# Gated output rows of both mixer branches by a seven-product scheme, with one weight sum made by an accumulating DMA

## The chip, the cores and the metric

The kernel runs on one core of one Trainium2 chip. The metric is the device time of one execution in microseconds; the time before is the median of 3 runs, 2480.94 us (2480.85 to 2481.19). The profile is of one more execution of the same program.

## The reference

Two layers of a streaming encoder for 640 frames (512 of a prompt, 8 x 16 of running streams), 1024 wide. What is computed in each layer:

```
x += 1/2 * SwiGLU_1(RMSNorm(x))
h  = RMSNorm(x);  z = h @ w_in        # conv B | conv C | conv V | q | k | v | gates
y_c = B * causal_depthwise_conv3(C * V)                 # 512 channels
y_a = chunk-band attention(q, k, v)                     # 8 heads x 64
m  = sigmoid(g_c) * (y_c @ w_conv_out) + sigmoid(g_a) * (y_a @ w_attn_out)
x += m @ w_o
x += 1/2 * SwiGLU_2(RMSNorm(x))
```

The part at issue is the line of m: the 2 x 1024 gate columns of h @ w_in, two products with 512-deep weights, and the gating.

## The kernel before, in words

Activations lie with channels on the 128 partitions and the 640 frames in the free dimension, as two halves t1 and t2 of 320. Each product of float32 matrices is made from three: each operand is split into a rounded "hi" part (a cast, on ScalarE) and the rest "lo" (a subtraction, on VectorE), and hi x hi, hi x lo and lo x hi are added up in PSUM. So each weight tile takes three matmuls of 320 columns for each half of the frames.

**Weights.** They come in slabs of 128 x 1024 (512 KB) from one packed tensor, wst. SP loads each into one of three buffers called raw (L292, in load). prep (L351) casts a slab to whi on ScalarE (L364) and leaves the subtraction for wlo pending; flush (L369) issues it on VectorE. A slab is prepared about two ahead of its use.

**Seven products.** A part of the products uses a Strassen-Winograd scheme on 2 x 2 blocks: seven block products in place of eight, with sums of weights and of activations as operands. A unit of it (kind "mix" in the plan) takes two raw slabs, ra and rb, and prepares four slabs of weights out of them (source, L302 on): ra whole; the sums s = (rb first half + rb second half) + ra first half, and rb's own sum, as one slab; then a sum that was *lent*, beside a changed second half of ra; then the second half of rb. A lent sum is made by DMA: lend_one (L278) has POOL load half of ra into a buffer called one (L281) and then, when that has landed, has POOL add half of rb onto it (L282, a DMA that accumulates). There are two such buffers. Units with a lent sum are called lean; in the others VectorE makes that sum as well. In the lean units VectorE makes rb's own sum first (raw<-raw), then s (s<-raw,raw).

**The order.** In this stage the instructions of TensorE, VectorE and ScalarE run in the order in which the program writes them; those of POOL and SP are placed by a scheduler, and each queue then runs in its order. A wait of one instruction holds everything behind it on its engine. In the function outputs (L1497 on) each layer goes through gate pairs (gate_pair, two rows of 128 gates, seven blocks of twelve matmuls) with output rows in between: `out` makes one row of 128 as a plain product (24 matmuls, PSUM tile py), rows makes four rows at once by seven products (84 matmuls, tiles raco, rbco, rcco or the like). The order is: gate pair 2, plain rows 0 to 3 of the convolution branch, gate pairs 4 and 6, its rows 4 to 7 by seven, gate pair 8, two plain rows of the attention branch, gate pair 10, two more, gate pairs 12 and 14, its rows 4 to 7 by seven, then the output projection (tile po).

A gate pair of name m uses PSUM tiles qa, qb, qc out of four such banks in turn, so the second tile of a gate pair takes the bank of the first tile of the gate pair ahead of it. Each block's result is copied out by ScalarE or added up by VectorE (g<-qb, g<-qa, g<-qc) and multiplied with the row norms (L1541, L1548, L1554); the sigmoids follow a unit later (L1354). `ahead` in a gate pair or in rows, behind the fifth block, makes the next unit's weight sums: there VectorE meets raw<-raw and s<-raw,raw.

The branch results y_c and y_a are split into hi and lo whole for the plain rows, and their sums for the seven products are made in further tiles (xhico, xhiao).

Of the kernel before, what the change touches and what calls it, by code (L numbers as in the profile page):

```python
# [16 lines left out]
P = 128  # L17
# [179 lines left out]
def trunk(ctx: ExitStack, tc: tile.TileContext, xin, wst, small, pbias, samplebias, kcache, vcache, gfin,  # L197
# [64 lines left out]
    lent, lean, at = {}, set(), 0  # L262
    for name, (_, units) in zip([f"{k}{l}" for l in range(L) for k in "amb"], stages()):
# [5 lines left out]
        lean.update(ns[slice(*LEAN.get(name, (FREE, None)))])  # L269

# [13 lines left out]
    def load(i):  # L284
        while len(raws) <= i:
# [6 lines left out]
            SP.dma_start(raw, wst[n])  # L292
        return raws[i]
# [8 lines left out]
    def source(i):  # L302
# [3 lines left out]
        if i not in sources:  # L306
# [8 lines left out]
            else:  # L315
# [8 lines left out]
                elif arg == 1 and n in lean:  # L324
# [4 lines left out]
                    add(rb[:, h1], rb[:, h1], rb[:, h2])  # L329
# [1167 lines left out]
    def outputs(l, gp, X, st, cs, ycp, yas, sigmoid, gates):  # L1497
# [4 lines left out]
        ycs = [z[:, i] for z in ycp for i in range(2)]  # L1502
        mm = [spare[i // 2][:, i % 2] for i in range(CT)] + ycs
# [14 lines left out]
        def gate_pair(m, at):  # L1518
# [6 lines left out]
            u, g = gates[m], gates[m + 1] = tmp(f"g{n}"), tmp(f"g{n}_1")  # L1525
            prep(used[0] + 1)
            flush()
            at[0]()
# [8 lines left out]
            at[1]()  # L1537
# [6 lines left out]
            at[2]()  # L1544
# [11 lines left out]
            flush()  # L1556

        def parts(pool, tag, name, src):
            hi, lo = (pool.tile([P, T], F32R, tag=f"{tag}{i}", name=f"{name}{i}") for i in ("hi", "lo"))
            split(hi, lo, src)  # L1560
            return hi, lo

        def out(m, y, then=None, post=None):

            due()
            py = acc(f"py{l}_{m}")
            product(py, y)
            if then:
                then()
            g = gates[m]  # L1570
            if m < KT:
                DVE.tensor_tensor(out=halves(mm[m]), in0=two(py), in1=halves(g), op=ALU.mult)
            else:
                DVE.tensor_tensor(out=halves(g), in0=two(py), in1=halves(g), op=ALU.mult)
                add(mm[m - KT], mm[m - KT], g)
            flush()
            if post:
                post()

        yc, ya = [], []  # L1580
        mo = [None] * KT
        srcs = [yas[:, c, :] for c in range(CT)]
        x, moves = {}, []

        def take(y, name, cs, srcs):
            for c in cs:
                y.append(parts(gp, f"y{c}", f"{name}{l}_{c}", srcs[c]))

        def take_even(c):
            y = tuple(gp.tile([P, T], F32R, tag=f"y{c}{i}", name=f"ya{l}_{c}{i}") for i in ("hi", "lo"))  # L1590
            split(*(z[:, t1] for z in y), srcs[c][:, t1])
            ya.append(y)

        def low(lo, z, hi):
            DVE.tensor_tensor(out=lo, in0=z, in1=hi.bitcast(F32), op=ALU.subtract)

        def room(name):
            for k in EXTRA:
                x[name, k] = tuple(gp.tile([P, 2, HT], F32R, tag=f"x{EXTRA.index(k)}{i}",
                                           name=f"x{i}{name}{l}_{EXTRA.index(k)}") for i in ("hi", "lo"))  # L1600

        def minus(out, a):
            DVE.scalar_tensor_tensor(out=out, in0=a, scalar=-1.0, in1=out, op0=ALU.mult, op1=ALU.subtract)

        def mixed(i):

            z = ycp[i].rearrange("p c (a b) -> p (c a) b", a=2)
            e1, e2, o1, o2 = (z[:, k] for k in range(4))
            add(e1, e1, e2, ALU.subtract)
            add(e2, o2, e2, ALU.subtract)  # L1610
            minus(o2, e1)
            minus(o1, o2)
            yield
            for k in EXTRA:
                ACT.copy(x["co", k][0][:, i], z[:, 1 + EXTRA.index(k)])
            yield
            for k in EXTRA:
                hi, lo = (u[:, i] for u in x["co", k])
                low(lo, z[:, 1 + EXTRA.index(k)], hi)
            yield  # L1620
            hi, lo = (u[:, t2] for u in yc[2 * i])
            ACT.copy(hi, e1)
            yield
            low(lo, e1, hi)
            yield

        za = yas.rearrange("p (i c) (a b) -> p i (c a) b", i=2, a=2)

        def mix(n):

            e1, e2, o1, o2 = (za[:, :, k] for k in range(4))
            if n == 0:
                add(e1, e1, e2, ALU.subtract)
            elif n == 1:
                add(e2, o2, e2, ALU.subtract)
            else:
                minus(*((o2, e1) if n == 2 else (o1, o2)))

        def place(k):
            if k == XT5:  # L1640
                return [(*(u[:, t2] for u in ya[2 * i]), za[:, i, 0]) for i in range(2)]
            return [(*x["ao", k], za[:, :, 1 + EXTRA.index(k)])]

        def high(*ks):
            for k in ks:
                for hi, _, z in place(k):
                    ACT.copy(hi, z)

        def rest(*ks):
            for k in ks:  # L1650
                for hi, lo, z in place(k):
                    low(lo, z, hi)

        EXTRA = XT7, XT4, XN6

        def kind(name, i, k):
            if k in EXTRA:
                return tuple(z[:, i] for z in x[name, k])
            hi, lo = (yc if name == "co" else ya)[2 * i + (k in (X21, X22))]
            return tuple(z[:, t2 if k in (X22, XT5) else t1] for z in (hi, lo))  # L1660

        def rows(name, ms, first, mid=None, late=None, end=False, defer=False):

            n = f"{name}{l}_{ms[0]}"
            gs = [gates[m + (KT if name == "ao" else 0)] for m in ms]
# [3 lines left out]
            s1, s2, s5 = stage  # L1669

            def mul(ps, s, half, k, start):
                for u in range(2):
                    for i in range(2):
                        kp = half * NP + 2 * u + i
                        wh, wl = (z[:, kp * P : (kp + 1) * P] for z in s)
                        xh, xl = kind(name, i, k)
# [13 lines left out]
            def moved(r):  # L1690
                for u in range(2):
                    ACT.copy(mm[ms[2 * r + u]], gs[2 * r + u])

            w = quiet()
            mul(a, w, 0, X11, True)
            ACT.copy(s1, two(A))
# [3 lines left out]
            if first:  # L1700
                first()
            mul(b, w, 1, X21, True)
            add(s1, two(B), s1)
            w = slab(True)[0]
            flush()
# [3 lines left out]
            if mid:  # L1709
                mid()  # L1710
# [728 lines left out]
```

## Time and profile before

| what | value |
|---|---|
| median of 3 runs | 2480.94 us |
| the profiled execution, its span | 2479.9 us |
| TensorE (PE) busy | 2466.4 us, 17264 matmuls recorded |
| VectorE (DVE) busy | 2182.6 us |
| ScalarE (ACT) busy | 1386.7 us |
| POOL busy | 320.8 us |
| the changed stage, layer 0 and layer 1 | 139.30 us and 139.38 us |

Busy time is a share of the whole span; a wait shows only in the stage in which it stands. In rows of the profile "out<-in" names the tile written and those read, "xN" counts instructions, and L364 is line 364 of the kernel. "idle before <-X" is how long the engine had waited, and for whom. A DMA's landing time counts from its issue. The granted clock of TensorE is 1.00 throughout.

### The profile page before, as it was taken

How to read it: one execution, taken by the hardware profiler on the slowest of the kernel's cores; microseconds unless marked ns; L12 is line 12 of the kernel's file. 1: busy time of each engine (PE TensorE's matmuls, PEld its weight loads, DVE VectorE, ACT ScalarE, POOL GpSimd, SP SyncE). 2: the span in 40 equal slices, each digit the busy share in tenths (PEclk: the TensorE clock that was granted, in tenths of full speed). 3: DMA queues.
4: the chain of work that ended last, by engine and by line, in shares of the span. 5: the costliest groups of instructions: out<-in, count | busy, mean ns of one | idle time of the engine just before them, and what ended most of it. 6: DMA issues, size and time to landing. Idle time of an engine off the chain costs nothing.

```text
span 2479.9 us, 44056 instructions
## 1 busy us (share of the span) xinstructions
PE 2466.4 (99%) x17264; PEld 2414.6 (97%) x17264; DVE 2182.6 (88%) x3644; ACT 1386.7 (56%) x2231; POOL 320.8 (13%) x483
## 2 busy tenths in 40 slices
PE   9999999999999999999999999999999999999999
PEld 8999999889999999999999999998899999999998
DVE  7999998888888899998799999988888889999997
ACT  6555555665555555555665555566655556555555
POOL 0211112211000001111001010121110000111111
PEclk9999999999999999999999999999999999999999
DMA  4443444335344234444334343452453432444444
GB/s 155 128 120 101 124 117 120 114 110 175 102 118 123 93 102 107 112 118 119 109 94 109 110 117 102 117 128 102 138 167 94 119 119 92 108 113 107 112 117 117
DMA packets 113520, 288.16 MB, mean 116 GB/s; under 512 B 12992, under 2 KB 52544, under 8 KB 113312
## 3 DMA queue, kind: packets, MB, share of 16 engines
q1 hardware_dynamic: 69552, 220.10, 27.0%
q0 software_dynamic: 43328, 64.99, 13.8%
q8 instruction: 135, 2.21, 0.4%
q14 instruction: 73, 0.60, 0.1%
q10 hardware_dynamic: 432, 0.25, 0.0%
HBM read 239.48 MB, written 7.94 MB: 100 GB/s over the span
## 4 chain that ended last, share of the span: by engine, by line
PE 91%; DVE 4%; issue 3%; ACT 1%; DMA 1%; DVEq 0%; SPq 0%; ACTq 0%; POOLq 0%
PE pab L459 12%; PE paa L459 10%; PE pcb L459 6%; PE daa L1147 5%; PE dab L1147 5%; PE pca L459 5%; PE po L435 5%; PE qa L459 4%; PE pbb L459 3%; PE dca L1147 3%; PE dcb L1147 2%; PE pba L459 2%; PE ma_cv L459 2%; PE ma_qk L459 2%; PE py L435 2%
## 5 line engine op out<-in xcount | busy, mean ns | idle before, releaser
L364 ACT CAST whi<-raw 128x1024 fp32r<-128x1024 f32 (+1 forms) x578 | 502.3, 874 | 373.4 <-PE pbb L459 46.3
L369 DVE TENSOR_TENSOR wlo<-raw,whi 128x1024 fp32r<-128x1024 f32 (+1 forms) x578 | 577.0, 1001 | 135.4 <-ACT whi L364 131.2
L364 ACT CAST whi<-s 128x1024 fp32r<-128x1024 f32 (+1 forms) x162 | 152.9, 944 | 319.4 <-DVE s L296 113.5
L459 PE MATMUL pab<-xhib,whi 128*128 128x320 f32 x704 | 217.7, 309 | 0.0
L459 PE MATMUL pab<-xhib,wlo 128*128 128x320 f32 x704 | 217.2, 309 | 0.0
L459 PE MATMUL pab<-xlob,whi 128*128 128x320 f32 x704 | 217.2, 309 | 0.0
L459 PE MATMUL paa<-xhia,whi 128*128 128x320 f32 x640 | 197.8, 309 | 0.2 <-DVE ga L296 0.2
L459 PE MATMUL paa<-xhia,wlo 128*128 128x320 f32 x640 | 197.5, 309 | 0.0
L459 PE MATMUL paa<-xloa,whi 128*128 128x320 f32 x640 | 197.5, 309 | 0.0
L369 DVE TENSOR_TENSOR wlo<-s,whi 128x1024 fp32r<-128x1024 f32 (+1 forms) x162 | 176.3, 1088 | 4.0 <-ACT whi L364 4.0
L1169 POOL DMA_DIRECT2D x<-c_a x80 | 69.9, 1021 | 575.9 <-ACT ahia L1051 205.5
L1169 POOL DMA_DIRECT2D x<-c_b x72 | 63.2, 1014 | 583.1 <-ACT ahib L1051 205.4
L459 PEld LDWEIGHTS pab<-xhib,whi 128*128 128x128 f32 x704 | 132.1, 188 | 0.9 <-issue 0.9
L459 PEld LDWEIGHTS pab<-xhib,wlo 128*128 128x128 f32 x704 | 132.1, 188 | 0.0
L459 PEld LDWEIGHTS pab<-xlob,whi 128*128 128x128 f32 x704 | 132.1, 188 | 0.0
L459 PEld LDWEIGHTS paa<-xhia,whi 128*128 128x128 f32 x640 | 120.1, 188 | 1.1 <-DVE ga L296 0.4
L459 PEld LDWEIGHTS paa<-xloa,whi 128*128 128x128 f32 x640 | 120.1, 188 | 0.3 <-DVE xloa L703 0.3
L459 PEld LDWEIGHTS paa<-xhia,wlo 128*128 128x128 f32 x640 | 120.1, 188 | 0.1
L296 DVE TENSOR_TENSOR raw<-s,raw 128x512 f32<-128x512 f32 x162 | 110.7, 683 | 0.0
L459 PE MATMUL pcb<-xhib,wlo 128*128 128x320 f32 x352 | 108.8, 309 | 0.0
L459 PE MATMUL pcb<-xlob,whi 128*128 128x320 f32 x352 | 108.6, 309 | 0.0
L459 PE MATMUL pcb<-xhib,whi 128*128 128x320 f32 x352 | 108.6, 309 | 0.0
(909 smaller groups left out, 8201.3 us busy)
## 6 DMA issues: line engine op xcount, KB each, us to landing
raw<-in_wst SPq DMA_DIRECT2D x375, 512.0 KB, 3.5
x<-c_a POOLq DMA_DIRECT2D x80, 160.0 KB, 4.8
x<-c_b POOLq DMA_DIRECT2D x72, 160.0 KB, 4.2
lent<-in_wst POOLq DMA_DIRECT2D x36, 256.0 KB, 3.7
kc<-in_kcache SPq DMA_DIRECT2D x32, 256.0 KB, 4.8
vc<-in_vcache SPq DMA_DIRECT2D x16, 512.0 KB, 4.3
one<-in_wst POOLq DMA_DIRECT2D x32, 256.0 KB, 4.0
x<-u_a POOLq DMA_DIRECT2D x40, 160.0 KB, 4.1
```

Source lines behind the costliest of these rows:

```text
L296: DVE.tensor_tensor(out=out, in0=a, in1=b, op=op)
L364: ACT.copy(hi[:, d], src[:, c])
L369: DVE.tensor_tensor(out=lo, in0=src, in1=hi.bitcast(F32), op=ALU.subtract)
L435: PE.matmul(ps[:, a, :HT], w, x[a] if isinstance(x, tuple) else x[:, a * HT : (a + 1) * HT], start=first and j == 0 and not seeded, stop=l ...
L459: PE.matmul(ps, a, b, start=start and kp == 0 and j == 0, stop=stop and kp == NP - 1 and j == 2, skip_group_check=True)
L1147: PE.matmul(ps[u], w, y, start=start and i == 0 and j == 0, stop=i == 1 and j == 2, skip_group_check=True)
L1169: POOL.dma_start(x[ms[2 * u + r]][:, cols], z[:, u], accum_op=ALU.add)
```

## The change

The plain product `out` goes. All rows of both branches are made by rows, four at a time: seven gate pairs (2 to 14) and four groups a layer, the groups behind gate pairs 4, 6, 10 and 14. That is eleven units a layer, ten of them lean (gate pair 2 is not), where there were nine units, eight of them lean, and eight plain rows. Gate pair 4 is now followed by a group, gate pair 2 directly by gate pair 4.

The operands of the seven products are made in place: a class Mixed holds, for each pair of 128 channels, the parts "11" (one), "21" and "22" (two) and T7, T5, T4, N6 (four); its steps are called at given places in the gate pairs and groups. Four gate results are now written to the tiles that hold m (mm, and the buffers of y_c) directly.

In a group, T5 (on the second stage's weights) now comes ahead of "21" (on the first stage's). But for the first group of each layer, the result of "11" is copied by ScalarE from its PSUM bank into the bank of "21", which then adds onto it; a VectorE addition of 640 columns goes.

For the lean units, rb's own sum is no longer made by VectorE: once rb has landed, POOL adds its second half (read anew from wst) onto its first half, in the raw buffer, by an accumulating DMA.

```diff
-    out += gates[:2] + [("co", m) for m in range(4)] + gates[2:4] + [("rows", ("co", (4, 5, 6, 7)))]
-    for i in range(2):
-        out += [gates[4 + i], ("ao", 2 * i), ("ao", 2 * i + 1)]
-    out += gates[6:] + [("rows", ("ao", (4, 5, 6, 7)))]
+    rows = [("rows", (name, ms)) for name in ("co", "ao") for ms in ((0, 1, 2, 3), (4, 5, 6, 7))]
+    out += gates[:3] + rows[:1] + gates[3:4] + rows[1:2] + gates[4:6] + rows[2:3] + gates[6:] + rows[3:]
...
+        if name[0] == "m":
+            added.update(n + 1 for n in ns[FREE:])
...
             SP.dma_start(raw, wst[n])
+            if n in added:
+                POOL.dma_start(raw[:, h1], wst[n][:, h2], accum_op=ALU.add)
...
-                    add(rb[:, h1], rb[:, h1], rb[:, h2])
                     add(st, rb[:, h1], ra[:, h1])
...
+        class Mixed:
...
+            def steps(self):
+                hi, lo, mix = self.high, self.low, self.mix
+                return ([lambda: (hi(0, "one", "two"), mix(0, "T5"), lo(0, "one"))],
+                        [lambda: (hi(1, "one", "two"), lo(0, "two"), mix(0, "N6"))],
+                        [lambda: (mix(0, "T4", "T7"), hi(0, "four"))],
+                        [lambda: mix(1, "T5")],
+                        [lambda: lo(1, "one")],
+                        [lambda: lo(0, "four")],
+                        [lambda: (lo(1, "two"), mix(1, "N6", "T4", "T7"), hi(1, "four"))],
+                        [lambda: lo(1, "four")])
...
             w = quiet()
-            mul(a, w, 0, X11, True)
-            ACT.copy(s1, two(A))
+            mul(a, w, 0, "11", True)
+            ACT.copy(two(B) if seed else s1, two(A))
...
-            mul(b, w, 1, X21, True)
-            add(s1, two(B), s1)
-            w = slab(True)[0]
-            flush()
-            mul(a, w, 0, XN6, False)
-            ACT.copy(s2, two(A))
-            gated(0, [s1[:, u] for u in range(2)], t1)
...
+            w1 = quiet()
+            mul(c, w1, 1, "T5", True)
+            for u in range(2):
+                ACT.copy(s5[:, u], c[u])
+            mul(b, w, 1, "21", not seed)
+            if not seed:
+                add(s1, two(B), s1)
+            gated(0, b if seed else [s1[:, u] for u in range(2)], t1)
+            prep(used[0] + 1)
+            flush()
+            mul(a, w1, 0, "N6", False)
+            ACT.copy(s2, two(A))
...
+        yc = Mixed("co", [quarters(z) for z in ycp])
+        at = yc.steps()
+        gate_pair(2, at[:4])
+        gate_pair(4, at[4:7])
+        rows(yc, (0, 1, 2, 3), at[7:])
+        gate_pair(6)
+        rows(yc, (4, 5, 6, 7))
+        ya = Mixed("ao", [quarters(yas[:, 2 * i : 2 * i + 2]) for i in range(2)])
+        at = ya.steps()
+        gate_pair(8, at[:4])
+        gate_pair(10, at[4:7])
+        rows(ya, (0, 1, 2, 3), at[7:])
```

VectorE's order at the end of gate pair 6 of layer 0, where the group of rows 4 to 7 follows, before (the raw slabs here are rb = raw_7820 and ra = raw_7800, and the waits are given in brackets, DMAHW for SP's transfers and DMASW for POOL's):

```order
L369 TENSOR_TENSOR wlo_7803<-raw_7800,whi_7802 128x1024 [waits DMAHW1_49,Activation_49]
L296 TENSOR_TENSOR raw_7820<-raw_7820 128x512 [waits DMAHW2_49]
L296 TENSOR_TENSOR s_100_7825<-raw_7820,raw_7800 128x512 [waits DVE_49]
L296 TENSOR_TENSOR g_6_7748<-qc_6_7732,capsm_4819 128x320 [waits PE_49]
L1548 TENSOR_TENSOR g_6_7748<-g_6_7748,rrm_4820 128x640 [waits DVE_49]
L1554 TENSOR_TENSOR g_6_1_7749<-qa_6_7730,rrm_4820 128x320 [waits PE_49]
L369 TENSOR_TENSOR wlo_7842<-s_100_7825,whi_7841 128x512 [waits Activation_49]
```

The same place now (rb = raw_7823, ra = raw_7803; gate pair 6 writes to the buffer of y_c):

```order
L370 TENSOR_TENSOR wlo_7806<-raw_7803,whi_7805 128x1024 [waits DMAHW1_49,Activation_49]
L298 TENSOR_TENSOR s_100_7829<-raw_7823,raw_7803 128x512 [waits DMAHW2_49,DMASW6_49]
L298 TENSOR_TENSOR yc_1_4822<-qc_6_7737,capsm_4819 128x320 [waits PE_49]
L1553 TENSOR_TENSOR yc_1_4822<-yc_1_4822,rrm_4820 128x640 [waits DVE_49]
L1559 TENSOR_TENSOR yc_1_4822<-qa_6_7735,rrm_4820 128x320 [waits PE_49]
L370 TENSOR_TENSOR wlo_7845<-s_100_7829,whi_7844 128x512 [waits Activation_49]
```

The sum raw<-raw is gone, and s now waits for a transfer of POOL's as well, at the same place in the order.

POOL's order around that place, before: the pairs of transfers that make lent sums, one behind the other.

```order
L281 DMA one_7691<-in_wst 128x512 [waits DMASW3_49,DVE_49]
L282 DMA one_7691<-in_wst 128x512 [waits DMASW5_49]
L281 DMA one_7822<-in_wst 128x512 [waits DMASW4_49,DVE_49]
L282 DMA one_7822<-in_wst 128x512 [waits DMASW7_49,DMASW0_49]
L281 DMA one_7954<-in_wst 128x512 [waits DMASW6_49,DVE_49]
```

And now:

```order
L281 DMA one_7692<-in_wst 128x512 [waits DMASW4_49,DVE_49]
L282 DMA one_7692<-in_wst 128x512 [waits DMASW1_49]
L294 DMA raw_7689<-in_wst 128x512 [waits DMAHW5_49,DMAHW2_49,DMAHW7_49,DMAHW0_49,DVE_49]
L281 DMA one_7826<-in_wst 128x512 [waits DMASW7_49,DVE_49]
L282 DMA one_7826<-in_wst 128x512 [waits DMASW5_49,DMASW4_49]
L294 DMA raw_7823<-in_wst 128x512 [waits DMAHW7_49,DMAHW2_49,DVE_49]
L281 DMA one_7957<-in_wst 128x512 [waits DMASW2_49,DVE_49]
```

Behind each pair stands the transfer (L294) that adds onto a raw slab: raw_7823 is the rb of the group above, and one_7826 the lent sum of the unit behind that group.

More of the change, by code (lines that the diff above doesn't have):

```diff
@@ L1516, in due, with call, gate_pair @@
             lates.clear()
-        def gate_pair(m, at):
+        def call(at, i):
+            if i < len(at):
+                for f in at[i]:
+                    f()
+        def gate_pair(m, at=()):
             n = f"{l}_{m}"
@@ L1524, in gate_pair @@
             due()
-            u, g = gates[m], gates[m + 1] = tmp(f"g{n}"), tmp(f"g{n}_1")
+            u, g = gates[m], gates[m + 1] = [mm[m + i] if m in (2, 6) else tmp(f"g{n}_{i}") for i in range(2)]
             prep(used[0] + 1)
             flush()
-            at[0]()
+            call(at, 0)
             block(pb, s0, 1, X21, every, True, True)
@@ L1556, in gate_pair @@
             flush()
[L1558 to L1575, printed above, removed]
-            flush()
-            if post:
-                post()
@@ L1580, in outputs @@
[L1580 to L1660, printed above, removed]
@@ L1666, in rows @@
+        seeded = [False]
+        def rows(y, ms, at=(), end=False):
+            n = f"{y.name}{l}_{ms[0]}"
+            co = y.name == "co"
+            gs = [gates[m + (0 if co else KT)] for m in ms]
             B, A = (acc(f"r{i}{n}") for i in "ba")
@@ L1718, in rows @@
             ahead()
-            if defer:
-                moves.append(lambda: gated(1, [s5[:, u] for u in range(2)], t2, -1.0))
-            else:
-                gated(1, [s5[:, u] for u in range(2)], t2, -1.0)
-            if late:
-                late()
-            mul(c, w, 1, X22, False)
+            gated(1, [s5[:, u] for u in range(2)], t2, -1.0)
+            call(at, 2)
+            mul(c, w, 1, "22", False)
             for u in range(2):
```

102 lines of the change are left out of this document (56 added, 46 removed).

## The prediction

> **What bounds the kernel now.** The page's head came first, then who waited for whom on TensorE.
>
> ```profile
> span 2479.9 us, 44056 instructions
> PE 2466.4 (99%) x17264; PEld 2414.6 (97%) x17264; DVE 2182.6 (88%) x3644; ACT 1386.7 (56%) x2231; POOL 320.8 (13%) x483
> ```
>
> ```profile
> PE poa L435 <- ACT whi L759: 5.6, 1, 5.6
> PE npsa L543 <- DVE ssuma L296: 0.6, 1, 0.6
> ```
>
> After the first load nothing holds TensorE for more than 0.6 us, so its matmuls are the time. Their price is in the chain that ended last, and the changed stage (from the second gate pair to the first product of the output projection) is in the windows, one row for each layer.
>
> ```profile
> 635.17 1.76 PE qa L459 x12
> 647.47 14.08 PE py L435 x96
> 774.47 56.36 PE po L435 x384
> ```
>
> ```profile
> core 0: us, PE busy (x) PEld busy (x) DVE busy (x) ACT busy (x) POOL busy (x), PEclk, DMA share, GB/s
> 635.17:774.47 139.30, 139.25 (x950) 138.95 (x950) 120.73 (x195) 79.73 (x133) 8.60 (x12) 1.00 0.36 106
> 1863.60:2002.98 139.38, 139.33 (x951) 139.03 (x950) 120.72 (x195) 79.72 (x133) 8.64 (x12) 1.00 0.35 107
> ```
>
> One matmul of 320 columns costs 14.08 / 96 = 146.7 ns, a block of twelve 1.76 us, and a unit (seven blocks) 12.32 us. VectorE is idle 18.6 us of 139.3. I then read VectorE's order in time where gate pair 6 goes over into a seven-product group and that into gate pair 8.
>
> ```profile
> 673.26 0.69 DVE L296 TENSOR_TENSOR s<-raw,raw 128x512 f32<-128x512 f32 x1
> 678.08 0.69 DVE L369 TENSOR_TENSOR wlo<-one,whi 128x512 fp32r<-128x512 f32 x1 [0.67 <-ACT whi L364]
> 678.69 0.69 DVE L369 TENSOR_TENSOR wlo<-raw,whi 128x512 fp32r<-128x512 f32 x1
> 684.84 0.68 DVE L296 TENSOR_TENSOR raw<-raw 128x512 f32<-128x512 f32 x1
> 685.56 0.69 DVE L296 TENSOR_TENSOR s<-raw,raw 128x512 f32<-128x512 f32 x1
> 687.43 0.48 DVE L1554 TENSOR_TENSOR g<-qa,rrm 128x320 f32<-128x320 f32 x1
> 690.70 0.69 DVE L369 TENSOR_TENSOR wlo<-one,whi 128x512 fp32r<-128x512 f32 x1 [0.98 <-ACT whi L364]
> 697.67 0.69 DVE L296 TENSOR_TENSOR s<-raw,raw 128x512 f32<-128x512 f32 x1
> 703.29 0.68 DVE L369 TENSOR_TENSOR wlo<-one,whi 128x512 fp32r<-128x512 f32 x1
> ```
>
> I call the end of wlo<-one a unit's *mark* (678.77 here). It frees a lent slab for POOL; the wlo<-raw behind it frees the buffer into which the next unit's second raw slab is loaded. VectorE reaches the sums of that slab 684.84 - 678.77 = 6.1 us after the mark.
>
> ```profile
> L292 SPq DMA_DIRECT2D raw<-in_wst x2: 327/328/328, 679.4 to 680.4; - x2
> DMA to landing us min/median/max: 4.8/4.9/5.0
> ```
>
> The slab, asked for at 679.4, lands at 684.3, half a microsecond before it is used. That is the whole cover.
>
> **The change, part by part.** *Matmuls.* Each of four groups (two a layer) goes from 96 matmuls to 84, so 24 go in each layer: 24 x 0.1467 = 3.52 us a layer, 7.04 us in all, if TensorE stays full.
>
> *VectorE's arithmetic.* Sixteen weight sums go, four more stages of weights and eight operand sets come; its order holds 24 instructions more.
>
> ```profile
> L369 DVE TENSOR_TENSOR wlo<-raw,whi 128x1024 fp32r<-128x1024 f32 x14 | 17.1, 1219 | 0.9 <-ACT whi L364 0.9
> L296 DVE TENSOR_TENSOR raw<-raw 128x512 f32<-128x512 f32 x9 | 6.1, 683 | 0.0
> L296 DVE TENSOR_TENSOR capsm<-rbco,capsm 128x640 f32<-128x640 f32 x1 | 0.8, 818 | 0.0
> ```
>
> By starts in the rows above (0.60 us for 512 columns, 1.05 ns a column) the additions and removals come to about +2.5 us a layer: 123 us of work in 135.5 us. That fits, so I cost it at nothing while VectorE isn't held. If the cover is gone it is the terms W below. The seeding copy (0.7 us on ScalarE) lies under the T5 block of 1.76 us that now follows X11: nothing too.
>
> *The weight sum by DMA.* VectorE's sum was 0.68 us. In its place a transfer adds 256 KB onto the slab, and it may start only when the slab has landed; on POOL's queue it stands behind the two transfers that make a lent slab, of which the second waits for the first. POOL's rows in this stage, by tile, and the two pairs with the longest and the shortest such wait:
>
> ```profile
> L281 POOL DMA_DIRECT2D one<-in_wst x6: 570/570/582, 666.9 to 740.9; - x6
> L282 POOL DMA_DIRECT2D one<-in_wst x6: 858/861/864, 670.6 to 745.3; - x6
>   DMA one<-in_wst: 21.9, 6
> DMA to landing us min/median/max: 2.9/4.0/5.2
> ```
>
> ```profile
> 679.17 0.57 POOL L281 DMA_DIRECT2D one<-in_wst  x1 [7.69 <-DVE wlo L369]
> 684.88 0.86 POOL L282 DMA_DIRECT2D one<-in_wst  x1 [5.13 <-DMA one<-in_wst]
> 723.23 0.57 POOL L281 DMA_DIRECT2D one<-in_wst  x1 [14.40 <-DVE wlo L369]
> 726.48 0.86 POOL L282 DMA_DIRECT2D one<-in_wst  x1 [2.68 <-DMA one<-in_wst]
> ```
>
> From mark to landed sum, call it A: 0.4 until the first of the pair is issued (678.77 to 679.17), 0.57 + 21.9/6 = 4.2 until the second, 0.86 for that, 4.0 for the added transfer's landing, and 0.35 for the signal (726.48 - 723.23 - 2.9). A = 9.8 us. The other chain gives the same without the queue: 0.6 to the slab's load, 4.9 landing, 4.0 and 0.35 again, 9.85. For the low end stands the shortest landing of an accumulating transfer here, that issued at 745.3:
>
> ```profile
> DMA to landing us min/median/max: 3.7/3.7/3.7
> ```
>
> With the shortest pair it gives 0.4 + 3.25 + 0.86 + 3.7 + 0.35 = 8.5. With the longest landing, 5.2, A is 11.0. I take 9.8, since four of its five terms are medians or means of this very stage.
>
> VectorE's instructions are in program order, so at 6.1 us it stands still for 3.7 us in front of s<-raw,raw. Queued behind it are the last gate products of the unit. The last one (687.43) releases the PSUM bank that TensorE needs for the second block of a following gate pair, and the splits after it make the weights of its second stage. TensorE waits for both.
>
> Then comes the work W from that sum to the next mark. By the rows above it is 678.77 - 673.26 = 5.5 us (gate pair to gate pair), 691.39 - 685.56 = 5.8 (gate pair to group) and 703.97 - 697.67 = 6.3 (group to gate pair). In three of the nine steps operands are made in place behind the sum, on ScalarE too:
>
> ```profile
> 674.06 0.62 ACT L364 CAST whi<-s 128x512 fp32r<-128x512 f32 x1 [4.06 <-DVE s L296]
> 675.99 1.55 ACT L1354 ACTIVATE g<-g,sm 128x640 f32<-128x640 f32 x2
> 677.44 0.61 ACT L364 CAST whi<-one 128x512 fp32r<-128x512 f32 x1
> ```
>
> ```profile
> L364 ACT CAST whi<-raw 128x1024 fp32r<-128x1024 f32 x15 | 15.8, 1053 | 2.9 <-PE qc L459 1.4 <-PE rcao L1678 1.4 <-DVE raw L296 0.2
> L1647 ACT CAST xhiao<-ya 128x640 fp32r<-128x640 f32 x3 | 2.1, 731 | 0.0
> L1354 ACT ACT_TABLE_LOAD x1 | 1.3, 1283 | 0.0
> ```
>
> The 1280-column cast there (1.3 us, from 1053 and 731) waits for three VectorE operations and stands ahead of whi<-s, so that cast starts 3.9 us after the sum and not 0.8; with the 0.5 us that ScalarE idled, W grows by 2.7 (twice), and with two operations by 1.5 (once). Sum of W: 3 x 6.3 + 2 x 5.8 + 5.5 + 2 x 8.5 + 7.0 = 60.0.
>
> A unit lasts A + W from mark to mark, or 12.32 if TensorE is slower. Nine steps a layer: 9 x 9.8 + 60.0 - 9 x 12.32 = 37.3 us of standing still. The first added unit costs some 4 us more (0 to 6): a table load, four sigmoids and that cast (1.3 + 2 x 1.55 + 1.3 = 5.7 us of ScalarE) now come right behind gate pair 2, with no plain product in between, and some 1.5 us of it was free. A layer: 37.3 + 4 - 3.5 = 37.8; both, 75.6. The profiled execution becomes 2479.9 + 75.6 = 2555.5; the median of the runs shown, 2480.94, lies 1.0 above its span, so 2556.5.
>
> The Trainium skill, "DMA: Bandwidth & Descriptors", section on the anatomy of one DMA, has 2.0 us plus bytes over 436 GB/s, an estimate of 2.6 us for 256 KB. The twelve landings here, 2.9 to 5.2, are all longer. By it A would be 6.8 and the sum 2502.
>
> **The rivals.** *The sum lands in time.* If A were 6.1 VectorE would not stop, TensorE would stay full, and the time is 2480.94 - 7.04 = 2473.9. For it: a TensorE at 99% and VectorE's 18.6 us of idle time. Against it: 8.5 from the shortest rows. It turns slower from A + W of about 12.7.
>
> *Only the first unit's backlog*, 4 us a layer, without the wait: 2473.9 + 8 = 2481.9.
>
> *Short landings*, because longer units leave the DMA engines freer. POOL's transfers of this size that meet little else land in
>
> ```profile
> out_vo<-v POOLq DMA_DIRECT2D x10, 256.0 KB, 2.7
> ```
>
> 2.7 us: A = 0.4 + 3.05 + 0.86 + 2.7 + 0.35 = 7.4, and with W at 5.9 (53.1 / 9, below) it is 2 x (9 x 1.0 - 3.5) = 11, so 2492. For it: a DMA share of 0.36. Against it: the same three transfers still start within 2 us of a mark.
>
> *Long landings*: A = 12.5 (0.4 + 5.7 + 0.86 + 5.2 + 0.35), 2 x (9 x 6.9 + 0.5) = 125, so 2606.
>
> *The clock falls* in the new gaps: granted 1.00 in both rows above, where no gap is. One block of twelve at half speed after each of 20 gaps, 1.76 us each, is 35 more: 2592, if TensorE is last there. The Trainium skill, "TensorE: Matmul & The Clock Gate", part 1 on the HAM clock gate, says that one idle window of about 3.4 us halves the clock; no run here shows it yet.
>
> **How the numbers follow.** Forecast 0.80; in time 0.05; backlog only 0.02; short 0.04; long 0.05; clock 0.04. Low end of the forecast: A = 8.5 and W without ScalarE's part (53.1), nothing for the first unit: 2 x (76.5 + 53.1 - 110.9 - 3.5) = 30, so 2511. High end: A = 11.0: 2 x (99 + 60 - 110.9 + 0.5) = 97, so 2578. What lies outside is 0.20, and the range is 2511 to 2578. About 0.2%, 5 us, is what a measurement of this kernel can tell. Faster 0.05, same 0.02 (2481.9 alone), slower 0.93.
>
> **What would show it.** Right: nine times a layer the wait for s<-raw,raw is put down to the accumulating transfer, 3 to 4 us each; unit lengths of 15 to 18 us; TensorE waiting for VectorE's gate products and splits; the stage at 177 us or so. Wrong: no such wait and a stage of 135.5 us (the cover holds), or a wait of 1 us (landings), or gaps on TensorE elsewhere. A granted clock below 1 would show the clock.

## The result, and the profile after

The changed kernel takes 2597.01 us, the median of 4 runs (2595.14 to 2600.33), where the kernel before took 2480.89 beside it (2480.62 to 2481.19): a ratio of 1.0469, 95% interval 1.0454 to 1.0483. It is slower by 116 us. The forecast was 2556, slower by 75, with a range of 2511 to 2578. The sign holds, and so does the wait that was named; the sum is 41 us too small, and about half of what is missing is not that wait. The profiled execution has a span of 2598.3 us.

The head of the page after, to be read against the same lines of before:

```profile
span 2598.3 us, 44120 instructions
PE 2499.3 (96%) x17216; PEld 2435.9 (94%) x17216; DVE 2188.9 (84%) x3668; ACT 1397.2 (54%) x2245; POOL 344.2 (13%) x511
```

There are 48 matmuls fewer, as forecast, and yet TensorE is busy for 33 us longer: matmuls became slower. The windows of the changed stage (again from the second gate pair to the first product of the output projection) say where. The columns are those of the windows shown of before.

```profile
core 0: us, PE busy (x) PEld busy (x) DVE busy (x) ACT busy (x) POOL busy (x), PEclk, DMA share, GB/s
635.17:832.53 197.36, 155.69 (x925) 149.79 (x924) 124.42 (x208) 85.20 (x140) 20.24 (x26) 0.87 0.38 94
1924.15:2121.51 197.36, 154.35 (x917) 148.69 (x916) 123.90 (x207) 84.86 (x139) 20.16 (x26) 0.87 0.38 95
```

The stage grew from 139.30 to 197.36 us, or 58.1; twice that is the whole 116. The forecast had 177 for it. VectorE has 73 us of idle time in it where it had 19, and the granted clock of TensorE is 0.87 where it was 1.00.

Who waited for whom, on TensorE over the whole span (before, one wait of 5.6 us and nothing else over 0.6):

```profile
PE qa L460 <- ACT capsm L1528: 23.9, 6, 5.4
PE rcco L1640 <- ACT whi L365: 20.2, 4, 6.1
PE rcao L1640 <- ACT whi L365: 13.4, 3, 6.5
PE rcao L1640 <- DVE y4ao_1lo L1595: 7.2, 2, 3.6
PE rcco L1640 <- DVE y4co_1lo L1595: 7.1, 2, 3.6
```

And what VectorE waited for in the stage of layer 0:

```profile
DVE s L298 <- DMA raw<-in_wst: 27.0, 8, 5.9
```

Eight times VectorE stands in front of s<-raw,raw for the transfer that now makes the weight sum, 3.4 us in the mean (3 to 4 were forecast; the single waits go from 0.3 to 5.9): in the first added unit, and in seven of the nine steps behind it. That is the wait that the prediction named, though it had it in all nine. How one step of it runs is seen at the place whose rows stand in the prediction, gate pair 6 into the group behind it. First VectorE, from one mark (the end of wlo<-one) to the next, then POOL, then two pieces of the chain that ended last: SP's load of the slab and the added transfer.

```profile
697.53 0.69 DVE L370 TENSOR_TENSOR wlo<-one,whi 128x512 fp32r<-128x512 f32 x1
710.42 0.69 DVE L298 TENSOR_TENSOR s<-raw,raw 128x512 f32<-128x512 f32 x1 [5.91 <-DMA raw<-in_wst]
712.29 0.48 DVE L1559 TENSOR_TENSOR yc<-qa,rrm 128x320 f32<-128x320 f32 x1
714.97 0.69 DVE L370 TENSOR_TENSOR wlo<-one,whi 128x512 fp32r<-128x512 f32 x1 [0.40 <-ACT whi L365]
```

```profile
698.58 0.57 POOL L281 DMA_DIRECT2D one<-in_wst  x1 [14.28 <-DVE wlo L370]
702.70 0.86 POOL L282 DMA_DIRECT2D one<-in_wst  x1 [3.56 <-DMA raw<-in_wst]
704.17 0.85 POOL L294 DMA_DIRECT2D raw<-in_wst  x1 [0.60 <-issue]
```

```profile
699.02 4.55 DMA raw<-in_wst
704.17 6.23 DMA raw<-in_wst
```

The mark is at 698.22. POOL starts the pair 0.4 us later, its second transfer 4.1 us after that, and the added transfer another 1.5 us on; it lands after 6.2, and VectorE goes on at 710.42, or 12.2 us after the mark. The forecast had 9.8 for this path, with 4.0 for the landing. In this step the chain runs through the load of the slab itself (landed at 703.57, the added transfer issued 0.6 us later) and not through the pair; so it does in five of the seven steps of this kind in layer 0. The prediction had that second path too, at 9.85, but without the 0.6. The gate product of 712.29 stands behind the wait, as forecast, and the next mark comes 5.2 us after the sum (5.8 was forecast for this step).

Read in this way from VectorE's rows, the nine steps of layer 0 have A, from mark to sum, of 10.93, 14.38, 12.20, 12.45, 10.73, 10.80, 13.67, 11.43 and 9.14 us (105.7 in all, forecast 88.2), and W, from sum to mark, of 58.9 in all (forecast 60.0). The added transfer's landings, grouped over the stage of layer 0 with those of the pairs (last column, median us to landing):

```profile
one<-in_wst POOLq DMA_DIRECT2D x16, 256.0 KB, 4.1
raw<-in_wst POOLq DMA_DIRECT2D x10, 256.0 KB, 5.1
```

One by one, and in both layers: the fifteen added transfers issued within about 1.5 us of a pair's second one landed after 5.0 to 6.5 us, the other five after 4.4 to 4.7. The 512 KB loads of the slabs were hardly slowed by the added traffic: their median landing in the stage of layer 0 is 4.5 us, and was 4.3 before.

The two longest values of A, 14.38 and 13.67, are not of this kind. They belong to the first group of each branch, and s<-raw,raw does not wait for the transfer there at all: TensorE is late. Its waits in the first of those groups:

```profile
674.33 0.64 PE L1640 MATMUL rcco<-y4co_0hi,whi 128*128 128x320 f32 x1 [5.37 <-ACT whi L365]
679.60 0.63 PE L1640 MATMUL rcco<-y4co_1lo,whi 128*128 128x320 f32 x1 [3.57 <-DVE y4co_1lo L1595]
687.90 0.41 PE L1640 MATMUL raco<-y4co_0hi,whi 128*128 128x320 f32 x1 [0.78 <-ACT rs L1674]
```

The first is T5, which now stands one block into the group and needs the second stage's weights at once; the second is the same block at the low part of its operand, which VectorE makes behind the weights; the third is T7, which stands right behind N6 in the same bank and must wait for ScalarE's copy of N6. Between the last two the chain shows the price of a block:

```profile
679.60 2.50 PE rcco L1640 x8
682.10 3.20 PE rbco L1640 x12
685.30 1.83 PE raco L1640 x12
```

Twelve matmuls took 3.20 us right behind the gaps, where before they took 1.76. The windows have it as clock; the first row below is this place, the second a place 12 us further on without a gap.

```profile
672.00:684.00 12.00, 6.11 (x20) 5.40 (x21) 6.11 (x9) 6.19 (x10) 2.02 (x3) 0.50 0.21 66
...
696.00:708.00 12.00, 11.52 (x79) 11.26 (x77) 6.02 (x11) 4.38 (x8) 2.29 (x3) 1.00 0.62 149
```

### The profile page after: what moved, and what is told of

Same layout as the page of the kernel before. It is cut to its first block, busy times and chain, and to the rows that moved or that the text cites. A ratio compares the mean times of both kernels' runs of the same rounds, so it can differ in the third digit from the quotient of the medians.

```text
span 2598.3 us, 44120 instructions
## 1 busy us (share of the span) xinstructions
PE 2499.3 (96%) x17216; PEld 2435.9 (94%) x17216; DVE 2188.9 (84%) x3668; ACT 1397.2 (54%) x2245; POOL 344.2 (13%) x511
## 4 chain that ended last, share of the span: by engine, by line
PE 80%; DVE 7%; DMA 6%; issue 3%; ACT 3%; POOL 0%; SPq 0%; DVEq 0%; POOLq 0%; ACTq 0%
PE pab L460 12%; PE paa L460 10%; PE pcb L460 6%; PE daa L1148 5%; PE pca L460 5%; DMA raw<-in_wst 5%; PE dab L1148 5%; PE po L436 4%; PE pbb L460 3%; PE dca L1148 3%; PE pba L460 3%; PE dcb L1148 2%; PE ma_cv L460 2%; PE ma_qk L460 2%; PE pv L1789 2%
```

## The experiments

The theory after the result, called D: the added transfer is what costs, since VectorE stands in program order in front of it, and the 41 us that were missed are a longer landing. Its rival, S: the new schedule costs by itself, because the operands are late and the blocks of a group stand in another order. A third, C: it is the clock. Nothing of the computation is left out in any of them; e7 has matmuls besides whose result nobody reads. Each time is a median of four runs, beside the kernel before, whose median in these sets was 2480.98 to 2481.11 us.

**e1, the transfer alone undone.** Everything else of the change stays.

```diff
-            if n in added:
-                POOL.dma_start(raw[:, h1], wst[n][:, h2], accum_op=ALU.add)
+                    add(rb[:, h1], rb[:, h1], rb[:, h2])
```

> The changed kernel with one part undone: rb's own weight sum is again made by VectorE and no transfer is added onto the raw slab. Theory D (the added transfer lands about 11 us after a unit's mark and VectorE stands in front of it): seven of the nine waits for the weight sum go, about 5 us each, in both layers; what is left is TensorE's wait for the T5 operands in the first group of each branch, 5 to 7 us each, and some 2 us at gate pair 4, so about 2481 - 7 + 2 x (12 + 2) = 2502, 2490 to 2515. Rival S (the new order and the operands made in place cost the time, and the transfer only shows as the last wait): 2560 to 2597.

Measured: 2540.04 us, ratio 1.0235 (1.0220 to 1.0250). Neither theory had this: of the 116 us, 57 go with the transfer, and 59 stay without it. S's part is as large as D's. TensorE's longest waits in e1:

```profile
PE rcao L1639 <- DVE y4ao_1lo L1594: 7.9, 2, 3.9
PE rcco L1639 <- DVE y4co_1lo L1594: 7.8, 2, 3.9
PE rcao L1639 <- ACT whi L364: 7.0, 4, 3.2
PE rcco L1639 <- ACT whi L364: 6.2, 2, 3.2
```

They are the waits of T5, with no transfer near.

**e2, the transfer alone made.** The kernel before, with its plain rows and its order, and the added transfer in its lean units.

```diff
+        if name[0] == "m":
+            added.update(n + 1 for n in ns[FREE:])
...
+            if n in added:
+                POOL.dma_start(raw[:, h1], wst[n][:, h2], accum_op=ALU.add)
...
-                    add(rb[:, h1], rb[:, h1], rb[:, h2])
```

> The kernel before with only that part added: in the eight lean units of a layer rb's own sum is made by the added transfer, all else as before. Theory D: units that follow plain rows have those 7 to 14 us as cover; the others pay, some 4 to 5 us at each of four or five steps a layer: 2481 + 36 = about 2517, 2505 to 2530. Rival S: 2478 to 2490, since VectorE does 16 sums less.

Measured: 2518.64 us, ratio 1.0156 (1.0141 to 1.0171), 37.6 us slower. D's working holds in size where the rest of the schedule is left alone. VectorE's waits in it, over the whole span, and then two of them in layer 0, the first between two seven-product units, the second where two plain rows lie in between:

```profile
DVE s L300 <- DMA raw<-in_wst: 46.2, 17, 5.6
```

```profile
676.42 0.69 DVE L300 TENSOR_TENSOR s<-raw,raw 128x512 f32<-128x512 f32 x1 [4.00 <-DMA raw<-in_wst]
727.37 0.69 DVE L300 TENSOR_TENSOR s<-raw,raw 128x512 f32<-128x512 f32 x1 [0.46 <-DMA raw<-in_wst]
```

They show what lead is worth. In the first three steps of the layer the kernel before reaches the sum 6.3 to 6.8 us after the mark; in e2 these wait 4.0, 5.4 and 4.3 us, and A is 10.7 to 10.9. In the two steps with plain rows the kernel before reaches it after 11.9 and 10.8 us; they wait 0.5 and 2.3.

**e3, the low part of the operand earlier.** e1 with the last step of the operands (the low part of T7, T5, T4 and N6 of the second half) at the end of the gate pair and not in the group that uses it.

```diff
-        gate_pair(4, at[4:7])
-        rows(yc, (0, 1, 2, 3), at[7:])
+        gate_pair(4, at[4:8])
+        rows(yc, (0, 1, 2, 3))
```

The same is done for gate pair 10 and the attention branch.

> As the run with the sum on VectorE, and the last operand step of each branch (the 1280-column low part, y4 low of the second pair) is made at the end of gate pairs 4 and 10, ahead of the first group's lent weights and not behind them. Theory T (TensorE also waits for that operand since T5 stands ahead of '21'): 2 to 3 us less in each of four groups than with the sum on VectorE alone, so 8 to 12 us less; what is left is the wait for the high part's cast. If the wait is only for weights: no change within 3 us.

Measured: 2526.78 us, ratio 1.0185 (1.0168 to 1.0202), 13.3 less than e1 and a little more than the 8 to 12 that were expected. The two waits for this operand fell from 15.7 us to 2.9, and hardly anything took their place:

```profile
PE rcao L1639 <- DVE y4ao_1lo L1594: 1.6, 2, 0.8
PE rcco L1639 <- DVE y4co_1lo L1594: 1.3, 2, 0.8
```

**e5, the same edit with the transfer kept** (the diff of e3, on the changed kernel).

> The changed kernel, the added transfer kept, with the same earlier low part. In the changed kernel's trace TensorE waits 3.6 us for y4 low in each of the two first groups and VectorE reaches the next sum 14 us after the mark there, against 11 elsewhere. Theory T: these two steps shrink to the 11 us of the others, 3 us each, four in all: 12 us less, about 2585. If the added transfer's wait is the whole loop everywhere: no change, since VectorE would then only wait longer for the transfer.

Measured: 2588.55 us, ratio 1.0433 (1.0417 to 1.0448), 8.5 less than the change, where 12 were expected. It is seen here too, though less than without the transfer.

**e6, the old order of the blocks.** e3, with a group's blocks in the order of the kernel before and without the seeding.

```diff
-            w1 = quiet()
-            mul(c, w1, 1, "T5", True)
-            for u in range(2):
-                ACT.copy(s5[:, u], c[u])
-            mul(b, w, 1, "21", not seed)
...
+            mul(b, w, 1, "21", True)
+            add(s1, two(B), s1)
+            w1 = quiet()
...
             mul(a, w1, 0, "N6", False)
             ACT.copy(s2, two(A))
...
+            mul(c, w1, 1, "T5", True)
+            for u in range(2):
+                ACT.copy(s5[:, u], c[u])
```

> Sum on VectorE, y4 low made early, and now the blocks of a group again in the order of before (11, 21, N6, T5, T7) with '21' in a bank of its own and VectorE adding it, so no seeding. Theory T (T5 on the second stage's weights 1.76 us into a group, where the kernel before needs them at 3.52, and N6 directly ahead of T7, which has to wait for N6's copy): the waits for the casts of those weights (about 3 us in five of the eight groups) and the four times two waits of 0.8 us for the copy go, with the slow clock behind them: 2527 - 2 x (6 + 3) - some 8 = about 2500, 2493 to 2512. Rival (the block order is free, what is left is VectorE's and ScalarE's total work): 2520 to 2530.

Measured: 2504.51 us, ratio 1.0092 (1.0077 to 1.0107), 22.3 less than e3. The waits of T5 for whi and of T7 for the copy of N6 are gone. The longest that are left, beside the 5.3 us at the start (5.6 in the kernel before):

```profile
PE qa L459 <- ACT capsm L1527: 5.8, 2, 2.9
...
PE raco L1639 <- ACT capsm L1657: 4.1, 2, 2.1
PE raao L1639 <- ACT capsm L1657: 4.0, 2, 2.0
```

**e11, the seeding apart from the order.** e3 with the seeding undone and T5 left ahead of 21.

```diff
-            seed = seeded[0]
+            seed = False
```

> e3 (weight sum on VectorE, low parts earlier, 2526.8 us) with the seeding alone undone: the result of block 11 goes to its buffer in every group, and VectorE adds 21 to it; T5 stays ahead of 21. Nothing is left out of the computation. Theory (it is the order, not the seeding, that costs the 22 us between e3 and e6): 2524 to 2532. Rival (the copy into the bank of 21 delays that block, or holds the bank): 2504 to 2515.

Measured: 2527.80 us (2527.04 to 2528.90), ratio 1.0190 (1.0173 to 1.0207), against 2525.93 to 2528.00 for e3. The seeding costs and gains nothing that can be measured here; the 22 us are the order's (in e6 the prep and the gated product move with the blocks).

**e10, the transfer with both mendings.** The change itself, with the edits of e3 and e6, so that it differs from e6 by the transfer alone.

> The change itself, added transfer included, with e6's two mendings: the low parts of the operands one unit earlier and the groups' blocks in the order of the kernel before, without seeding (it differs from e6 by the transfer alone, and from e5 by the block order alone). Nothing is left out of the computation. Theory F (with the transfer in the chain every step lasts as long as the pair, the transfer and the VectorE work behind it; the block order lies under that wait): the order's 22 us are hardly seen, 2578 to 2589. Rival P (the two costs lie behind one another): e5 less 22 = 2566, or e6 plus 57 = 2561; 2556 to 2570.

Measured: 2576.66 us, ratio 1.0385 (1.0370 to 1.0401). It lies between: 11.9 below e5 (theory F had 0 to 10, rival P 22), and 72.2 above e6. So the transfer is worth 57 us with the change's own order, 62 with the earlier low part (e5 against e3) and 72 with both mendings: the faults hide one another in part. VectorE's wait for the transfer over the whole span rose as the rest was mended; first the change's row, then e10's:

```profile
DVE s L298 <- DMA raw<-in_wst: 56.1, 18, 5.9
```

```profile
DVE s L298 <- DMA raw<-in_wst: 75.0, 21, 5.6
```

Some 19 us more of VectorE's time went into this wait when TensorE was less late. By VectorE's rows of layer 0, A sums to 99.5 us in e5 and to 98.3 in e10, where the two long ones of the change are 10.9 each; W stays at 59.1 and 59.4. But the 72 us hold another cost: the low part of the operand of block "21" is made behind the sum that waits, and with the old order of the blocks TensorE waits for it (3.5 us at most). e6 has no such wait.

```profile
PE rbao L1640 <- DVE y2ao_1lo L1595: 5.7, 2, 3.5
PE rbco L1640 <- DVE y2co_1lo L1595: 4.1, 2, 2.1
```

**e7, the gaps filled.** The change, with 48 matmuls of 192 columns behind the first block of each lean gate pair and each group, into unread columns of the same bank.

```diff
             mul(a, w, 0, "11", True)
+            for i in range(48):
+                PE.matmul(A[:, 0, HT:], w[0][:, :P], y.kind(0, "11")[0][:, : 512 - HT], start=False, stop=True,
+                          skip_group_check=True)
```

Gate pairs have the like behind their first block.

> The changed kernel with work added: 48 matmuls of 192 columns behind the first block of each lean unit, into columns of that block's bank that nothing reads, about 4 us of TensorE in each gap. Theory C (the gaps make the clock fall to half, and that is part of the time): the granted clock goes back towards 1.00 and the kernel gets faster by 5 to 25 us although it does 80 us more of matmuls. Rival (the loop of transfer, sum and splits sets the pace and the slow clock hides beside it): clock up, time the same within 5 us or longer by up to 20, as the filling delays the copy of the first block.

Measured: 2625.86 us, ratio 1.0580 (1.0564 to 1.0596). The clock over the span rose from 0.98 to 0.992, and the time grew by 29 us, more than the 20 that the rival allowed. It settles little: the filling delays the copy of the first block on ScalarE, and with it, as I read it, the weights behind that copy. The longest wait of wlo for whi, in the change and then in e7:

```profile
DVE wlo L370 <- ACT whi L365: 150.3, 123, 3.3
```

```profile
DVE wlo L370 <- ACT whi L365: 185.3, 131, 5.2
```

So the experiment brought a fault of its own, and what the clock costs by itself can't be told from it.

**e8, the groups moved away from their operands.** e6 with gate pairs 2, 4, 6 first and then both groups of the convolution branch, so that a gate pair lies between operands and use; the sigmoids of a unit go behind the casts of the weights.

```diff
-    out += gates[:3] + rows[:1] + gates[3:4] + rows[1:2] + gates[4:6] + rows[2:3] + gates[6:] + rows[3:]
+    out += gates[:4] + rows[:2] + gates[4:6] + rows[2:3] + gates[6:] + rows[3:]
...
-            due()
             u, g = gates[m], gates[m + 1] = [mm[m + i] if m in (2, 6) else tmp(f"g{n}_{i}") for i in range(2)]
             prep(used[0] + 1)
+            due()
```

The second group swaps its two banks, and the sigmoids move in the groups too.

> As the run with the old block order, and the convolution branch's two groups both stand behind gate pair 6 (so one more unit lies between the last operand and its use), and the sigmoids of a unit come behind the casts of its lent weights. By the theories so far what is left after the old block order is the late operands and the late lent weights at gate pair 4: about 5 us a layer less, 2480 to 2495; if all gaps close, 2474. Rival (VectorE's work in the stage, about 123 us in 135, doesn't fit with its waits for TensorE's results): no better than the run with the old block order.

Measured: 2514.46 us, ratio 1.0131 (1.0114 to 1.0148), worse than e6 by 10. The expectation failed. New waits stand in the place of the old: gate pairs wait for a copy that is now behind the sigmoids (first row), and the second group for a bank of the first (second row).

```profile
PE qa L459 <- ACT capsm L1538: 8.8, 8, 1.6
...
PE raco L1641 <- DVE mm L1650: 5.1, 2, 2.6
```

**e9, two sigmoids later.** e6 with the sigmoids of gate rows 0 and 1 at the end of gate pair 4.

```diff
-            if m == 2:
+            if m == 4:
                 for i in range(2):
                     sigmoid(gates[i], i)
```

> e6 (the old block order in the groups, weight sum on VectorE, 2504.5 us) with one move: the sigmoids of gate rows 0 and 1, issued at the end of gate pair 2, are issued at the end of gate pair 4. Nothing is left out of the computation. Theory (the first added unit is late because ScalarE's table load and four sigmoids stand ahead of its casts): e6's two longest single waits, 2.9 us each for ScalarE's copy of a gate pair, go, and the time falls by 4 to 10 us, to 2494 to 2500. Rival (the wait is only moved to gate pair 4, since the sigmoids hold the casts there as well): 2502 to 2507.

Measured: 2499.26 us, ratio 1.0072 (1.0057 to 1.0087), 5.2 less than e6. The wait of gate pair 4 for capsm L1527 is gone, and the one of the first convolution group rose from 2.1 to 3.7 us each, since those sigmoids now stand ahead of its copy. The time is in the theory's range; a part of the wait only moved, as the rival had it, though to another place:

```profile
PE raco L1639 <- ACT capsm L1657: 7.4, 2, 3.7
```

**e12, ScalarE's way cleared.** e6 with the two sigmoids in the middle of gate pair 4, and the 1280-column cast of the last operand behind the casts of the weights.

```diff
             ACT.copy(c5, pc)
+            if m == 4:
+                for i in range(2):
+                    sigmoid(gates[i], i)
...
-                        [lambda: (lo(1, "two"), mix(1, "N6", "T4", "T7"), hi(1, "four"))],
-                        [lambda: lo(1, "four")])
+                        [lambda: (lo(1, "two"), mix(1, "N6", "T4", "T7"))],
+                        [lambda: (hi(1, "four"), lo(1, "four"))])
```

> e6 (old block order, low parts earlier, weight sum on VectorE, 2504.5 us) with two moves on ScalarE that clear its way in front of the first group of each branch: the sigmoids of gate rows 0 and 1 go into gate pair 4, behind the copy of its fourth block, where ScalarE was idle; the cast of 1280 columns of the last operand goes behind the casts of the weights, to the end of the gate pair. Nothing is left out of the computation. Theory (what is left of e9's 18 us over the kernel before is TensorE waiting at the start of these groups for ScalarE's copy, 3.7 and 2.0 us, and the granted clock of 0.80 behind that wait): the copy's waits fall below 1 us and the time to 2484 to 2493. Rival (the operand or the weights take the place of the copy as what comes last): 2495 to 2502. Faster than the kernel before by neither.

Measured: 2493.90 us (2493.12 to 2499.64), ratio 1.0050 (1.0033 to 1.0067). That is just above the theory's range, and short of the rival's. It is the best of these kernels and still slower than the one before. The profiled execution is the longest of the four, 2499.64 us, so these waits are those of a run 5.7 us above the median. In it the copy's waits fell, but not quite below 1 us, and those for the operand rose from 0.8 us each (e6) to 1.4, as the rival had it:

```profile
PE raao L1639 <- DVE y4ao_1lo L1594: 2.9, 2, 1.4
PE raco L1639 <- DVE y4co_1lo L1594: 2.9, 2, 1.4
...
PE raco L1639 <- ACT capsm L1657: 2.5, 2, 1.2
```

Behind those waits the clock is on the chain that ended last. The place in the first convolution group of layer 0:

```profile
667.79 2.50 PE raco L1639 x8
670.30 3.20 PE rcco L1639 x12
673.50 1.97 PE raco L1639 x12
```

These 32 matmuls take 7.67 us where 4.69 is the full rate (32 x 0.1467), and those of the attention branch's first group 7.65: 6 us lost in layer 0, about as much as the 6.4 us that TensorE waits there.

The change with more lead for the transfer (the rb slab in a buffer of its own, loaded a unit earlier) wasn't tried; what lead does is seen in e2 alone.

## Why the prediction was right in kind and wrong in size

**The mechanism held.** VectorE stands in front of s<-raw,raw for the accumulating transfer, 3.4 us in the mean; gate products and splits queue behind it; TensorE waits for copies and weights that come behind those. e2, the transfer alone, came to 37.6 us, and taking it out of the change gives back 57.

**W held**: 58.9 us against 60.0. The 2.7 us that the 1280-column cast was to add to two of the steps are there: these two are 8.53 and 8.52, and 8.5 was forecast.

**The step that failed is A.** In layer 0 it measured 105.7 us (in layer 1, read in the same way, 104.7), not 88.2. Two faults of about equal weight stand behind the miss.

- *The landing.* In the seven steps that end with the transfer, A is 11.1 in the mean; in e10, where the other fault is mended, 10.9 over all nine. That is 1.1 to 1.3 above 9.8 in each; most of it is the landing, and some 0.3 a later start (0.5 in the step shown). The step said 4.0, which is the median over all twelve transfers of the pairs before; the six that accumulate had 4.3 by themselves, and the added ones have 4.4 to 4.7 with no pair just ahead of them and 5.0 to 6.5 behind one. So the price was that of a transfer of another kind, in part, and at another place in the queue. Nor were four of the five terms medians or means, as the prediction says: 0.4 and 0.35 are single rows. Nine steps in two layers at 1.1 make 20 us.
- *What was costed at nothing.* T5 ahead of 21, and the low part of an operand made behind the wait. The text priced the arithmetic of VectorE, and the seeding copy under the T5 block, but never asked when T5 itself can start. The two long steps, 14.38 and 13.67, come from this: in e1, without the transfer, A is 14.13 and 13.87 in the same two steps. Undoing both takes 20.4 us out of the change (e10), and 35.5 out of it where there is no transfer (e6 against e1).

The ledger of a layer: A 17.5 more than forecast, W 1.1 less. The first and the last unit together, as what remains of 58.05 after 105.7 + 58.9 - 110.9 - 3.5, make 7.9 where the first had 4; in e10 the same working gives between 4 and 5. So 17.5 - 1.1 + 3.9 = 20.3, and twice that is 40.6 of the 41 missed. It closes because that last term is a remainder; A and W are measured.

**The base was too good as well.** A step was to last 12.32 us wherever the transfer doesn't bind. In e6, without the transfer and with both mendings, nine steps take 121.6 us by the marks, 10.7 more than 110.9, and the kernel is 23.4 us over the one before; the forecast's working had 1 for it (8 for the two first units less 7.04). This does not add to the miss, because the transfer's wait covers it. But it says that the rivals "in time" (2473.9) and "backlog only" (2481.9) could not have come true by the transfer's speed alone: with no transfer at all e1 takes 2540.04 us. e12 shows that 10.6 of the 23.4 lie in ScalarE's order in front of the first groups.

**The rivals.** "Long landings" (2606) is the nearest to 2597, and had the right term; that it comes so near is luck in part, since it had 5.2 for the pair's transfer too and nothing for the order of the blocks. "The clock falls" is half right: 0.87 in the stage, 0.50 at worst. Along the chain, the 32 matmuls behind 679.60 took 7.53 us where 4.69 is the full rate, so that place lost 2.8 us to it; it lies inside the long A of 14.38. The same place of the attention branch (from 773.35) took 6.84, or 2.2 more than 4.69. That makes about 5 us of slow matmuls on the chain in layer 0, so the clock is a small part of the 58 there. How much it does off this chain isn't settled: e7 couldn't tell, and every mending that removed gaps raised the clock with them.

**The seeding** costs nothing that can be measured, as forecast (e11).

**The pages named.** The Trainium skill, "DMA: Bandwidth & Descriptors", anatomy of one DMA, would have given an estimate of 2.6 us for 256 KB; the medians here are 4.1 and 5.1, so the measurement decides against it for these transfers. The Trainium skill, "TensorE: Matmul & The Clock Gate", part 1, has the clock halved by one idle window of about 3.4 us; the gaps of 5.37 and 3.57 us with a granted clock of 0.50 around them agree. The time of one window isn't a lower bound in these traces: in e12 gaps of 1.23 and 1.44 us, with 0.9 us of matmuls in between, are followed by 5.8 us in which matmuls start 0.27 us apart and not 0.147. The prediction said that no run showed the halving yet, but the trace of before does: behind the wait of 5.56 us at the start, matmuls start 0.27 us apart until 10.6 us, although the granted clock in that window reads 1.00.

## What to carry to other kernels

A scheme with fewer matmuls must bring its operands and weights earlier, not only cheaper: for each block that moves forward, look up when its weights, both parts of its operand and its bank are ready in the profile of before. A DMA put in the place of a cheap vector operation costs its whole landing, and all that queues behind the waiting instruction, unless something gives it lead (in e2 two plain rows in between did); price it by a transfer of the same kind at the same place of the queue. And where several faults lie in one chain, undo them one at a time and all together: here the price of the same transfer was 57, 62 or 72 us, according to what else was late.

## What the runs showed of the hardware

The accumulating transfer of 256 KB landed in 5.1 us in the median, where plain ones and accumulating ones of the pair, on the same queue and in the same stage, had 4.1; behind a pair it took 5.0 to 6.5, and 4.4 to 4.7 elsewhere. TensorE's granted clock is lowered by gaps of a few us, in e12 by two of 1.23 and 1.44 close together, and shows in the time of the blocks behind them: in the change 3.20 us for twelve matmuls, then 1.83, where a block takes 1.76 in the kernel before.
